# A hybrid attention block on one core: ln_g as columns, memory keys and values stored unsplit, decay sums as strips

## The chip, the cores and the metric

The kernel runs on one core of a Trainium2 chip. The metric is the device time of one execution in microseconds. Runs are compared as medians; the profile is of one further execution, taken by the hardware profiler, which has its own time. The engines are named as the profile names them: PE is TensorE (PEld its weight loads), DVE is VectorE, ACT is ScalarE, POOL is GpSimd, SP is SyncE, which only issues DMAs here.

## What is computed

One layer of a decoder over 1024 tokens of width 2048, in float32:

```
h = RMSNorm(x) * ln_g
P = h @ W_in            split into g_u g_v g_z | d_q d_k d_v d_z d_a d_b | c_q c_z
A: gMLP gating in chunks of 128;  B: gated DeltaNet, 8 heads;  C: attention into 256 memory tokens, 4 heads
m = RMSNorm(mem) * mem_norm_g;  mk, mv = split(m @ w_mem_kv)
x = x + concat(A, B, C) @ W_out;  y = RMSNorm(x) * final_g
```

Two small pieces matter here. The columns d_a and d_b of W_in are 16 in all (8 heads, two numbers for each); with them every token gets its decay and its beta: `g = -exp(a_log) * softplus(d_a + dt_bias)`, `beta = sigmoid(d_b)`. And mk, mv are made once at the start and used in the cross-attention much later, so they are stored in between.

## The kernel before

A float32 product is made of three products in the faster type fp32r: an operand is split into a high part (a cast) and a low part (the difference), and hi*hi, hi*lo and lo*hi are added in PSUM (`triple`, line 445; `split_to`, line 437, the cast on ACT and the subtraction on DVE). Transposes and a few small products use plain fp32.

The whole program is first recorded as operations (`Plan.add`, line 138) and then put in order by a planner (`Plan.issue`, line 229): each engine has a queue of what is ready, takes the lowest rank (`with rank(...)`), and prices each operation by a model (`price`, line 188). Which operation waits for which follows from the regions that they write and read (`region`, line 108); a PSUM bank counts as one region. Each engine runs its own instructions in the planned order, so all recorded lines of the trace are line 300, and groups are told apart by the names of the tiles. `together` (line 102) keeps a bundle of PE instructions in one piece. `behind(op)` makes an operation wait for another.

**Opening.** Rows of mem (256 tokens) and the first half of x (token tiles 0 to 3 of 128 tokens) are loaded with tokens in partitions, four blocks of 512 columns for a tile. `row_scale` (line 454) makes the RMS factor of each token: four squares with a running sum on ACT, 512 columns each, then DVE and POOL. `prep` (line 546) multiplies a block by that factor and by ln_g in one DVE instruction (line 551). For that ln_g lies in SBUF as four broadcasts over all partitions (`gb`, line 479, loaded at line 605 from SP's queue). PE transposes the block into a PSUM bank of the ring dn. `put0` (line 559) takes it from there: for tiles 0 and 1 ACT copies it to SBUF, it is split into `ahq`/`alq`, and the sum is written to `h0_d` in DRAM; for tiles 2 and 3 it is split straight from PSUM, and the sum is made again later from both parts and written then (`whole`, line 728, and `left_sums`, line 734).

Between these steps runs the product of the memory (lines 580 to 633): for each of 16 k, a block of w_mem_kv is loaded, scaled and split, and PE makes keys (`ka`, four banks acc0 to acc3, 256 columns each) and values (`va`, banks dn0 and dn1). At its end (lines 635 to 658) keys and values are scaled, split, and both parts stored to `kv_d` by POOL's queue.

**Tiles 4 to 7** are prepared while the first large product already runs (lines 1322 to 1333): `prep1` (line 747) leaves the transposed block unsplit in SBUF, writes part of it to `hT_d`, and `left_sums` forms sums of first and second half. Large products over 2048 columns of P follow in the rest of the program; they are made from sums of blocks, seven products for eight, in the order of `first_product` and `seven`.

**Decays.** `abw` holds the 16 columns of W_in, split into two parts of 16 columns for each k. For the second half (tiles 4 to 7) `decay_rows` (line 781) puts the 16 values of k into four strips: four fp32 matmuls with a 32-column stationary operand write to partitions 0, 32, 64 and 96 of one bank, 16 matmuls for a token tile, in one bundle. For the first half `decay_mm` (line 776) multiplies all 512 tokens with the split operands, 32 matmuls with 512 columns (lines 1326 to 1330). `decays` (line 793) transposes the result, adds the groups and makes gates and decays.

**Late.** In the cross-attention stage (lines 1733 to 1737) keys and values are read from `kv_d` in both parts, from POOL's queue, into tiles of the rings gt and inv.

Of the kernel before, what the change touches and what calls it, by code (L numbers as in the profile page):

```python
# [17 lines left out]
P = 128  # L18
D = 2048
KT = D // P  # L20
NQ = 4
# [39 lines left out]
class Plan:  # L61
# [242 lines left out]
def kernel(  # L304
# [95 lines left out]
    et = [C([P, HT], f"et{i}", F32R) for i in range(2)]  # L400
    for t in et:
        R.users[t.tensor.name] = []
    ring = {t: Slots(t, 2, [P, HT]) for t in ("kT", "qT", "vs", "kd", "ai")}
    twin = {t: C([P, 2 * HT], f"{t}w") for t in ring}
    ring |= {t: Slots(t, 2, [P, 2 * HT]) for t in ("inv", "gt")}
    ring["ut"] = Ring("ut", 2, [P, 2 * HT])
    ring["zg"] = Ring("zg", 2, [P, 2 * HT])
    zgb = ring["zg"].bufs
    ring["zg"].bufs = [b[:, i * HT : (i + 1) * HT] for b in zgb for i in range(2)]
# [4 lines left out]
    jk = C([P, HT], "jk", mybir.dt.bfloat16)  # L414
# [64 lines left out]
    gb = [ring["zg"]() for _ in range(4)]  # L479
    kvraw += [ring["ut"]() for _ in range(2)]  # L480
    mem_rows = [row_tiles("kT"), row_tiles("qT")]
    x_rows = {}

# [21 lines left out]
    with rank(2):  # L505
        load_mem(0)
        S.dma_start(mrow, mem_norm_g[0].rearrange("(c p) -> c p", p=P))
        for k in range(4):
            load_kv(k)
            if k == 1:  # L510
                load_mem(1)
# [18 lines left out]
    pt = spare()  # L530
    PE.transpose(pt[:, 0:16], mrow, ident[0:16, 0:16])
    gcol = C([P, 16], "gcol")
    with rank(1):
        V.tensor_copy(gcol, pt[:, 0:16])
# [11 lines left out]
    def prep(tt, put, bank, order=range(NQ)):  # L546
# [30 lines left out]
    kvmark = []  # L577
    mhl = [spread_mem(0)]
    warm(2)
    for k in range(KT):  # L580
# [5 lines left out]
        with rank(2):  # L586
            for sl in kv_parts(k):
# [7 lines left out]
        for h in range(NX):  # L595
            sl = slice(h * P, (h + 1) * P)
            triple(ka[h][:, :NMEM], (hi[:, sl], lo[:, sl]), (mh[:, kk], ml[:, kk]), k == 0, k == KT - 1)
        for mt in range(2):
            sl = slice(mt * P, (mt + 1) * P)
            triple(va[mt], (mh[:, kk, sl], ml[:, kk, sl]), (hi[:, XW:], lo[:, XW:]), k == 0, k == KT - 1)  # L600
        kvmark.append(R.ops[-1])
        if k == 3:
            with rank(2), behind(kvmark[-1]):
                for c in range(4):
                    Q.dma_start(gb[c], ln_g[0, c * HT : (c + 1) * HT].partition_broadcast(P))
# [29 lines left out]
    kv_d = DT([2, NX, P, 2, NMEM], "kvd")  # L635
    with rank(1):
        kfs = [t[:, i * NMEM : (i + 1) * NMEM] for t in (ring["xr"](), ring["xr"]()) for i in range(2)]
        for h in range(NX):
            V.tensor_tensor(out=kfs[h], in0=ka[h][:, :NMEM], in1=rmb, op=ALU.mult)
    for mt in range(2):  # L640
        t = [ring[("ai", "kd")[mt]](F32R) for _ in range(2)]
        with rank(1):
            S.activation(t[0], va[mt], AF.Copy, scale=rm[mt])
            V.scalar_tensor_tensor(t[1], va[mt], rm[mt], t[0], op0=ALU.mult, op1=ALU.subtract)
        for i in range(2):
            with rank(2.5):
                G.dma_start(
                    kv_d[1, :, :, i, mt * P : (mt + 1) * P].rearrange("h p e -> p h e"),
                    tok(t[i]).bitcast(F32),
                )  # L650
    with rank(2):
        prep(3, put0(3), spare, (2, 3, 0, 1))
    for h in range(NX):
        t = (ring["vs"](F32R) if h < 2 else et[h - 2]).rearrange("p (s m) -> p s m", s=2)
        with rank(2.2):
            split_to(t[:, 0], t[:, 1], kfs[h], V)
        with rank(2.5):
            G.dma_start(kv_d[0, h], t.bitcast(F32))
    et = [heir(t, f"ef{i}", f"et{i}", HT) for i, t in enumerate(et)]


    R.gate = kvmark[8]
    with rank(2.5):
# [4 lines left out]
        abf = ring["E"]()[:, 0 : KT * 16].rearrange("p (k c) -> p k c", c=16)  # L668
        G.dma_start(abf, w_in[:, C_AB : C_AB + 16].rearrange("(k p) c -> p k c", p=P))
# [7 lines left out]
    with rank(3.5):  # L677
# [9 lines left out]
        abw = C([P, KT * 32 + 96], "abw", F32R)  # L687
        R.users[abw.tensor.name] = []
        V.tensor_scalar(abw[:, KT * 32 :], ident[:, 0:96], 0.0, None, op0=ALU.mult)
        abv = abw[:, 0 : KT * 32].rearrange("p (k c) -> p k c", c=32)  # L690
        S.copy(abv[:, :, 0:16], abf)
        V.tensor_tensor(out=abv[:, :, 16:32], in0=abf, in1=abv[:, :, 0:16], op=ALU.subtract)
# [35 lines left out]
    def whole(q, tt):  # L728
        t = ring["tn"]()
        with rank(4):  # L730
            V.tensor_tensor(out=tok(t), in0=ahq[q][:, tt], in1=alq[q][:, tt], op=ALU.add)
            Q.dma_start(rows_of(h0_d, q, tt), twos_of(t))

    def left_sums(tt, q):
# [4 lines left out]
        if tt >= H0:  # L739
            Q.dma_start(rows_of(h0_d, q, tt), twos_of(a))  # L740
# [6 lines left out]
    def prep1(i):  # L747
        def put(q, tp):
            t = x_rows[NT + i][q]
            S.copy(t, tp.rearrange("p t c -> p (t c)"))  # L750
# [30 lines left out]
    def decay_rows(o, tt):  # L781

        a = work()
        with R.together():
            for q in range(NQ):
                for j in range(4):
                    k = 4 * q + j
                    PE.matmul(a[j * 32 : (j + 1) * 32, 0:P],
                              abw[:, k * 32 : (k + 1) * 32].bitcast(F32), tok(x_rows[NT + tt][q])[:, j],
                              start=q == 0, stop=q == NQ - 1)  # L790
        S.copy(o[:, tt * P : (tt + 1) * P], a[:, 0:P])

    def decays(hf, a, bank):

        NU, M = NT * NH, P if hf else 32
# [7 lines left out]
        with rank(R.cls):  # L803
            V.tensor_reduce(abt, tp[:, 0 : NT * M].rearrange("p (t g c) -> p t c g", t=NT, c=2 * NH), axis=AX.X, op=ALU.add)
# [427 lines left out]
    def right_first(m, j):  # L1232

        ts = kept1[j]
        if m == 1:
            with rank(3.3):
# [82 lines left out]
    strips, sums0 = ring["xr"].bufs[2][:, 0:HT], ring["xr"].bufs[1][0:32, 0:HT]  # L1319
    room = over([*spares.bufs, *et])  # L1320
    R.slow = 800.0
    with rank(4):
        for i in range(NT):
            prep1(i)
            decay_rows(strips, i)
            if i == 1:
                a = work()
                for k in range(KT):
                    decay_mm(a, k)
                S.copy(sums0, a[0:32])  # L1330
# [3 lines left out]
    for q in range(NQ // 2, NQ):  # L1334
        for tt in range(H0, NT):
            whole(q, tt)
# [29 lines left out]
    zh, zl = (heir(b, n, tag, 2 * HT, F32R) for b, n, tag in zip(zgb, ("zh", "zl"), ("zg0", "zg1")))  # L1366
# [4 lines left out]
    el = over([heir(abw, "el0", "abw", KT * 32 + 96)[:, 0:HT], ring["tn"].bufs.pop()])  # L1371
# [444 lines left out]
    def square(half_, t, c):  # L1816
        S.activation(jk, ys[half_][t][c], AF.Square, accum_out=ssy[half_][t][:, c : c + 1])
# [108 lines left out]
```

## Time and profile before

| | |
|---|---|
| median of 3 runs | 1592.1 us (1588.9 to 1592.44) |
| the profiled execution | 1596.31 us, its span 1594.5 us |
| granted TensorE clock in it | 0.998 |
| busy: PE, DVE, ACT, POOL | 1576.7, 1291.9, 1017.2, 311.8 us |
| moved by DMA | 428.88 MB, mean 269 GB/s |

A row of instructions gives its start, its busy time, engine, line, operation, the tiles written and read, shape and count; in brackets how long the engine stood idle before it and what ended that. Busy time of overlapping instructions is counted once in a group. A row of waits gives who waited for whom: total, times, longest. A row of DMA issues gives the queue, the count, the size of one and the median time from issue to landing.

### The profile page before, as it was taken

How to read it: one execution, taken by the hardware profiler on the slowest of the kernel's cores; microseconds unless marked ns; L12 is line 12 of the kernel's file. 1: busy time of each engine (PE TensorE's matmuls, PEld its weight loads, DVE VectorE, ACT ScalarE, POOL GpSimd, SP SyncE). 2: the span in 40 equal slices, each digit the busy share in tenths (PEclk: the TensorE clock that was granted, in tenths of full speed). 3: DMA queues.
4: the chain of work that ended last, by engine and by line, in shares of the span. 5: the costliest groups of instructions: out<-in, count | busy, mean ns of one | idle time of the engine just before them, and what ended most of it. 6: DMA issues, size and time to landing. Idle time of an engine off the chain costs nothing.

```text
span 1594.5 us, 25290 instructions
## 1 busy us (share of the span) xinstructions
PE 1576.7 (99%) x8538; PEld 1324.7 (83%) x8538; DVE 1291.9 (81%) x1977; ACT 1017.2 (64%) x2115; POOL 311.8 (20%) x514
## 2 busy tenths in 40 slices
PE   9999999999999999999999999999999999999997
PEld 8878888888888888888888888888888888888886
DVE  6978986989899998998987776767778788778776
ACT  7843675776656788866776667665646874344355
POOL 1200132332302423245232233221000000000001
PEclk9999999999999999999999999999999999999999
DMA  9988868988679868986779775799877679688646
GB/s 331 326 288 269 289 202 294 360 297 270 203 248 343 276 216 279 351 311 221 263 233 343 249 272 180 232 309 327 298 243 240 225 236 360 202 277 293 215 148 242
DMA packets 214819, 428.88 MB, mean 269 GB/s; under 512 B 23193, under 2 KB 58737, under 8 KB 214689
## 3 DMA queue, kind: packets, MB, share of 16 engines
q1 hardware_dynamic: 191184, 368.71, 68.9%
q0 software_dynamic: 22896, 57.50, 10.8%
q8 instruction: 67, 1.10, 0.3%
q10 hardware_dynamic: 608, 1.06, 0.2%
q14 instruction: 64, 0.52, 0.1%
HBM read 337.49 MB, written 89.16 MB: 268 GB/s over the span
## 4 chain that ended last, share of the span: by engine, by line
PE 90%; DMA 5%; DVE 2%; issue 1%; ACT 1%; POOL 0%; SPq 0%; POOLq 0%; DVEq 0%; ACTq 0%
PE acc L300 63%; PE dn L300 27%; DMA wraw<-in_w_in_dram 2%; DVE wlo L300 1%; DMA kT<-late 1%; DVE alo L300 0%; DMA ut<-in_w_mem_kv_dram 0%; DMA qTw<-in_x_dram 0%; DMA qTw<-sa 0%; DMA vsw<-sa 0%; DMA kTw<-in_w_in_dram 0%; SPq L300 0%; DMA wraw<-in_w_mem_kv_dram 0%; ACT whi L300 0%; DMA y<-in_w_in_dram 0%
## 5 line engine op out<-in xcount | busy, mean ns | idle before, releaser
L300 PE MATMUL acc<-ahi,whi 128*128 128x512 f32 (+1 forms) x1328 | 458.5, 393 | 0.3 <-ACT whi L300 0.3
L300 PE MATMUL acc<-ahi,wlo 128*128 128x512 f32 (+1 forms) x904 | 354.2, 392 | 0.7 <-DVE wlo L300 0.7
L300 PEld LDWEIGHTS acc<-ahi,whi 128*128 128x128 f32 x1328 | 248.3, 188 | 48.0 <-ACT whi L300 0.5
L300 ACT CAST ahi<-raws 128x1024 fp32r<-128x1024 f32 x141 | 147.8, 1048 | 82.5 <-PE dn L300 35.9
L300 PEld LDWEIGHTS acc<-ahi,wlo 128*128 128x128 f32 x904 | 170.1, 188 | 33.6 <-DVE wlo L300 1.4
L300 PE MATMUL acc<-alo,whi 128*128 128x512 f32 (+1 forms) x480 | 187.4, 390 | 0.0
L300 PE MATMUL acc<-ahi,zh 128*128 128x512 f32 x424 | 167.1, 394 | 0.0
L300 PE MATMUL acc<-ahi,zl 128*128 128x512 f32 x424 | 166.9, 394 | 0.0
L300 PE MATMUL acc<-alo,zh 128*128 128x512 f32 x424 | 166.7, 393 | 0.0
L300 ACT CAST whi<-wraw 128x1024 fp32r<-128x1024 f32 (+1 forms) x78 | 80.6, 1034 | 68.8 <-PE acc L300 37.2
L300 POOL TENSOR_TENSOR small<-small,mhalf 128x1 f32<-128x1 f32 x26 | 16.9, 658 | 507.2 <-DVE small L300 507.1
L300 DVE TENSOR_TENSOR wlo<-wraw,whi 128x1024 fp32r<-128x1024 f32 (+1 forms) x78 | 93.9, 1204 | 25.1 <-ACT whi L300 19.4
L300 DVE TENSOR_TENSOR alo<-raws,ahi 128x1024 fp32r<-128x1024 f32 x71 | 86.6, 1219 | 22.6 <-ACT ahi L300 22.4
L300 PEld LDWEIGHTS acc<-alo,whi 128*128 128x128 f32 x480 | 90.3, 188 | 16.8
L300 DVE TENSOR_TENSOR ahi<-raws,ahi 128x1024 fp32r<-128x1024 f32 x70 | 85.4, 1219 | 20.9 <-ACT ahi L300 19.4
L300 ACT CAST ahi<-y 128x1024 fp32r<-128x1024 f32 x65 | 68.2, 1049 | 42.2 <-PE dn L300 17.8
L300 DVE TENSOR_TENSOR alo<-y,ahi 128x1024 fp32r<-128x1024 f32 x65 | 79.7, 1225 | 16.6 <-ACT ahi L300 16.5
L300 PEld LDWEIGHTS acc<-ahi,zl 128*128 128x128 f32 x424 | 79.7, 188 | 15.8
L300 PEld LDWEIGHTS acc<-ahi,zh 128*128 128x128 f32 x424 | 79.9, 188 | 15.4
L300 PEld LDWEIGHTS acc<-alo,zh 128*128 128x128 f32 x424 | 79.7, 188 | 15.3
L300 PE MATMUL dn<-whi,ahi 128*128 128x512 f32 x232 | 77.6, 389 | 0.0
L300 PE MATMUL acc<-whi,ahi 128*128 128x512 f32 x216 | 73.7, 392 | 0.0
(587 smaller groups left out, 3765.7 us busy)
## 6 DMA issues: line engine op xcount, KB each, us to landing
wraw<-in_w_in_dram SPq DMA_DIRECT2D x80, 512.0 KB, 5.4
raws<-sa SPq DMA_DIRECT2D x61, 512.0 KB, 5.2
y<-in_w_in_dram SPq DMA_DIRECT2D x40, 512.0 KB, 5.6
wraw<-in_w_out_dram SPq DMA_DIRECT2D x32, 512.0 KB, 5.2
raws<-h0d SPq DMA_DIRECT2D x29, 512.0 KB, 5.5
y<-sa SPq DMA_DIRECT2D x27, 512.0 KB, 5.0
raws<-sd SPq DMA_DIRECT2D x42, 256.0 KB, 3.0
raws<-hTd SPq DMA_DIRECT2D x16, 512.0 KB, 4.7
```

The source lines that it names most:

```text
L300: o.fn(*o.args, **o.kw)
```

## The change

- **ln_g as columns.** The four broadcasts and their tiles (`zg`) go. ln_g is loaded as 16 rows beside mem_norm_g, transposed with it, and kept as 16 columns in `gcol`. `prep` multiplies a block by the token's factor alone, on DVE for tiles 2 and 3 and on ACT for the others; the transposed block is multiplied by ln_g where it leaves PSUM (`times_g`, on DVE). Tiles 2 and 3 now take the way of tiles 0 and 1, so `h0_d` is written in `put0` for all four, and `whole` and the store in `left_sums` go.
- **Decays of the first half in strips.** `abw` is plain fp32, 16 columns for each k, loaded at the start of the key and value loop. Tiles 0 and 1: strips of four matmuls for each block, from `put0`, into columns 256 to 383 of the banks acc0 and acc1, beside the keys. Tiles 2 and 3: `decay_split`, 32 fp32 matmuls over 256 columns, from both split parts. Tiles 4 to 7: the strips of each block are a bundle of their own. PSUM banks named acc are tracked by columns.
- **Keys and values unsplit in DRAM.** `kv_d` has half its size; the split is made after the late fetch.
- **Squares 1024 wide** where two blocks of a tile are neighbours in SBUF.
- Smaller: half of the first weight block is issued from ACT; the halves of that block come in the other order, and values are multiplied before keys; the first fetches for product 1 wait for the twelfth step of the memory product; `zh`, `zl` and `et` are tiles of their own.

```diff
-        if ap.space == PSUM:
+        if ap.space == PSUM and name[:3] != "acc":
             return name, 0, P, 1
...
+    def joined(ts):
+        out, i = [], 0
+        while i < len(ts):
+            w = whole_of.get(ts[i].tensor.name)
+            out.append(ts[i] if w is None else w)
+            i += 1 if w is None else 2
+        return out
+
     def row_scale(xq):
         s = small()
-        for c in range(4):
-            S.activation(jk, xq[c], AF.Square, accum_out=s[:, c : c + 1])
-        V.tensor_reduce(s[:, 4:5], s[:, 0:4], axis=AX.X, op=ALU.add)
+        parts = joined(xq)
+        for c, t in enumerate(parts):
+            S.activation(jk[:, 0 : t.shape[1]], t, AF.Square, accum_out=s[:, c : c + 1])
+        V.tensor_reduce(s[:, 4:5], s[:, 0 : len(parts)], axis=AX.X, op=ALU.add)
...
-        for sl in kv_parts(k):
-            Q.dma_start(kvraw[k % 4][:, sl], w_mem_kv[k * P : (k + 1) * P, sl])
+        for i, sl in enumerate(kv_parts(k)[::-1]):
+            (S if (k, i) == (0, 0) else Q).dma_start(kvraw[k % 4][:, sl], w_mem_kv[k * P : (k + 1) * P, sl])
...
+    def times_g(o, tp, q):
+        V.tensor_tensor(out=o, in0=tp, in1=bc(gcol[:, 16 + 4 * q : 20 + 4 * q], P), op=ALU.mult)
...
-            V.scalar_tensor_tensor(xq[q], xq[q], r, gb[q], op0=ALU.mult, op1=ALU.mult)
+            if H0 <= tt < NT:
+                V.tensor_scalar(xq[q], xq[q], r, None, op0=ALU.mult)
+            else:
+                S.activation(xq[q], xq[q], AF.Copy, scale=r)
...
+    def first_ab(tt):
+        return ka[tt][:, NMEM : NMEM + P]
+
+    def decay_rows(a, q, t, start):
+        with R.together():
+            for j in range(4):
+                k = 4 * q + j
+                PE.matmul(a[j * 32 : (j + 1) * 32], abw[:, k * 16 : k * 16 + 32], t[:, j],
+                          start=start, stop=q == NQ - 1, skip_group_check=True)
+
     def put0(tt):
         def put(q, tp):
-            if tt >= H0:
-                with rank(1):
-                    split_to(ahq[q][:, tt], alq[q][:, tt], tp, V)
-                return
             t = tok(ring["tn"]())
             with rank(1):
-                S.copy(t, tp)
+                times_g(t, tp, q)
             with rank(2):
                 split_to(ahq[q][:, tt], alq[q][:, tt], t, V)
+            if tt < H0:
+                decay_rows(first_ab(tt), q, t, False)
...
-    kv_d = DT([2, NX, P, 2, NMEM], "kvd")
+    kv_d = DT([2, NX, P, NMEM], "kvd")
...
-    def decay_mm(a, k):
-        wk = abw[:, k * 32 : k * 32 + P]
-        mm(a, wk, ahi[k], k == 0, False)
-        mm(a, wk, alo[k], False, k == KT - 1)
...
+    def decay_split():
+        a = work()[:, 0 : H0 * P]
+        with R.together():
+            for i, part in enumerate((ahi, alo)):
+                for q in range(NQ):
+                    for j in range(4):
+                        k = 4 * q + j
+                        PE.matmul(a[j * 32 : (j + 1) * 32], abw[:, k * 16 : k * 16 + 32],
+                                  part[k][:, H0:].bitcast(F32), start=i == q == 0, stop=i == 1 and q == NQ - 1)
+        S.copy(sums0[:, H0 * P :], a)
...
             prep1(i)
-            decay_rows(strips, i)
+            a = work()[:, 0:P]
+            for q in range(NQ):
+                decay_rows(a, q, tok(x_rows[NT + i][q]), q == 0)
+            S.copy(strips[:, i * P : (i + 1) * P], a)
             if i == 1:
-                a = work()
-                for k in range(KT):
-                    decay_mm(a, k)
-                S.copy(sums0, a[0:32])
+                decay_split()
...
-            G.dma_start(t, kv_d[n, 2 * i : 2 * i + 2].rearrange("h p s m -> p h s m"))
+            G.dma_start(t[:, :, 1].bitcast(F32), kv_d[n, 2 * i : 2 * i + 2].rearrange("h p m -> p h m"))
+            with rank(1.5):
+                split_to(t[:, :, 0], t[:, :, 1], t[:, :, 1].bitcast(F32), V)
```

More of the change, by code (lines that the diff above doesn't have):

```diff
@@ L399 @@
     kvhi, kvlo = [*whi.bufs], [*wlo.bufs]
-    et = [C([P, HT], f"et{i}", F32R) for i in range(2)]
-    for t in et:
-        R.users[t.tensor.name] = []
+    et = [C([P, HT], f"et{i}") for i in range(2)]
     ring = {t: Slots(t, 2, [P, HT]) for t in ("kT", "qT", "vs", "kd", "ai")}
     twin = {t: C([P, 2 * HT], f"{t}w") for t in ring}
+    whole_of = {t.tensor.name: t for t in twin.values()}
     ring |= {t: Slots(t, 2, [P, 2 * HT]) for t in ("inv", "gt")}
     ring["ut"] = Ring("ut", 2, [P, 2 * HT])
-    ring["zg"] = Ring("zg", 2, [P, 2 * HT])
-    zgb = ring["zg"].bufs
-    ring["zg"].bufs = [b[:, i * HT : (i + 1) * HT] for b in zgb for i in range(2)]
     ring["E"] = Ring("E", 2, [P, HT])
@@ L478 @@
     R.late = R.LATE
-    gb = [ring["zg"]() for _ in range(4)]
     kvraw += [ring["ut"]() for _ in range(2)]
@@ L482 @@
     x_rows = {}
+    whole_of.update((t.tensor.name, t) for t in ring["ut"].bufs)
     def load_mem(q):
@@ L507 @@
         S.dma_start(mrow, mem_norm_g[0].rearrange("(c p) -> c p", p=P))
+        S.dma_start(rows[16:32], ln_g[0].rearrange("(c p) -> c p", p=P))
         for k in range(4):
@@ L529 @@
     warm(7)
-    pt = spare()
-    PE.transpose(pt[:, 0:16], mrow, ident[0:16, 0:16])
-    gcol = C([P, 16], "gcol")
+    pt = acc[3]
+    PE.transpose(pt[:, 0:32], rows[0:32], ident[0:32, 0:32])
+    gcol = C([P, 32], "gcol")
     with rank(1):
-        V.tensor_copy(gcol, pt[:, 0:16])
+        V.tensor_copy(gcol, pt[:, 0:32])
+    def times_g(o, tp, q):
+        V.tensor_tensor(out=o, in0=tp, in1=bc(gcol[:, 16 + 4 * q : 20 + 4 * q], P), op=ALU.mult)
     def spread_mem(q):
@@ L577 @@
     kvmark = []
+    abw = C([P, HT], "abw")
+    G.memset(abw[:, KT * 16 : KT * 16 + 16], 0.0)
     mhl = [spread_mem(0)]
@@ L586 @@
         with rank(2):
-            for sl in kv_parts(k):
+            for sl in kv_parts(k)[::-1]:
                 raw = kvraw[k % 4][:, sl]
@@ L600 @@
             triple(va[mt], (mh[:, kk, sl], ml[:, kk, sl]), (hi[:, XW:], lo[:, XW:]), k == 0, k == KT - 1)
+        for h in range(NX):
+            sl = slice(h * P, (h + 1) * P)
+            triple(ka[h][:, :NMEM], (hi[:, sl], lo[:, sl]), (mh[:, kk], ml[:, kk]), k == 0, False)
         kvmark.append(R.ops[-1])
[L602 to L605, printed above, removed]
+        if k == 0:
+            with behind(kvmark[-1]), rank(2):
+                G.dma_start(abw[:, 0 : KT * 16].rearrange("p (k c) -> p k c", c=16),
+                            w_in[:, C_AB : C_AB + 16].rearrange("(k p) c -> p k c", p=P))
         if k in (1, 4, 8):
@@ L633 @@
                 prep(2, put0(2), spare, (2, 3, 0, 1))
-    kv_d = DT([2, NX, P, 2, NMEM], "kvd")
+    kv_d = DT([2, NX, P, NMEM], "kvd")
     with rank(1):
-        kfs = [t[:, i * NMEM : (i + 1) * NMEM] for t in (ring["xr"](), ring["xr"]()) for i in range(2)]
+        kfs = [t[:, i * NMEM : (i + 1) * NMEM] for t in et for i in range(2)]
         for h in range(NX):
             V.tensor_tensor(out=kfs[h], in0=ka[h][:, :NMEM], in1=rmb, op=ALU.mult)
+    for h in range(NX):
+        with rank(2.5):
+            G.dma_start(kv_d[0, h], kfs[h])
     for mt in range(2):
-        t = [ring[("ai", "kd")[mt]](F32R) for _ in range(2)]
+        t = ring[("ai", "kd")[mt]]()
         with rank(1):
[L643 to L650, printed above, removed]
+            S.activation(t, va[mt], AF.Copy, scale=rm[mt])
+        with rank(2.5):
+            G.dma_start(kv_d[1, :, :, mt * P : (mt + 1) * P].rearrange("h p e -> p h e"), tok(t))
     with rank(2):
         prep(3, put0(3), spare, (2, 3, 0, 1))
[L653 to L659, printed above, removed]
+    sums0 = ring["xr"].bufs[1][:, 0:HT]
+    with rank(2):
+        for tt in range(H0):
+            S.copy(sums0[:, tt * P : (tt + 1) * P], first_ab(tt))
     R.gate = kvmark[8]
@@ L686 @@
             V.tensor_copy(col2, pt[:, 96:105])
[L687 to L692, printed above, removed]
     states = C([P, NH * P], "states")
@@ L726, in blk @@
         return w[k * P : (k + 2) * P, c0 : c0 + HT].rearrange("(u p) c -> p u c", u=2)
[L728 to L732, printed above, removed]
     def left_sums(tt, q):
@@ L749, in put @@
             t = x_rows[NT + i][q]
-            S.copy(t, tp.rearrange("p t c -> p (t c)"))
+            times_g(tok(t), tp, q)
             if q >= NQ // 2:
@@ L774 @@
     scan_banks, work = dnr.bufs[0:2], over(dnr.bufs[2:4])
-    def decay_mm(a, k):
-        wk = abw[:, k * 32 : k * 32 + P]
-        mm(a, wk, ahi[k], k == 0, False)
-        mm(a, wk, alo[k], False, k == KT - 1)
-    def decay_rows(o, tt):
-        a = work()
-        with R.together():
[L785 to L791, printed above, removed]
+    def decay_split():
+        a = work()[:, 0 : H0 * P]
+        with R.together():
+            for i, part in enumerate((ahi, alo)):
[5 more added lines that the diff above has]
+        S.copy(sums0[:, H0 * P :], a)
     def decays(hf, a, bank):
-        NU, M = NT * NH, P if hf else 32
+        NU, M = NT * NH, P
         ab = a
@@ L1235, in right_first @@
         if m == 1:
-            with rank(3.3):
+            with rank(3.3), behind(kvmark[11]):
                 fetch(ts, first_block(0, 0, j))
@@ L1318 @@
                     Q.dma_start(tiles[i][c], x[(NT + i) * P : (NT + i + 1) * P, c * HT : (c + 1) * HT])
-    strips, sums0 = ring["xr"].bufs[2][:, 0:HT], ring["xr"].bufs[1][0:32, 0:HT]
+    strips = ring["xr"].bufs[2][:, 0:HT]
     room = over([*spares.bufs, *et])
@@ L1365 @@
     wraw2 = over([*kvraw[:2], more[1]])
[L1366 removed]
+    zh, zl = (C([P, 2 * HT], n, F32R) for n in ("zh", "zl"))
     whi3, wlo3 = over([*kvhi, zh]), over([*kvlo, zl])
@@ L1370 @@
     cross = over([heir(b, f"utc{i}", f"ut{i}", 2 * HT, F32R) for i, b in enumerate(ring["ut"].bufs)])
-    el = over([heir(abw, "el0", "abw", KT * 32 + 96)[:, 0:HT], ring["tn"].bufs.pop()])
+    el = over([abw, ring["tn"].bufs.pop()])
     wide = acc
```

17 lines of the change are left out of this document (3 added, 14 removed).

## Prediction

> **What bounds the kernel now.** I read the page first, then the waits of TensorE, then the opening by windows, because every edit but one acts there.
>
> ```profile
> span 1594.5 us, 25290 instructions
> PE 1576.7 (99%) x8538; PEld 1324.7 (83%) x8538; DVE 1291.9 (81%) x1977; ACT 1017.2 (64%) x2115; POOL 311.8 (20%) x514
> ```
> ```profile
> PE dn L300 <- ACT vs L300: 1.7, 1, 1.7
> PE dn L300 <- DVE whi L300: 1.4, 1, 1.4
> ```
> ```profile
> PE dn L300 <- ACT jk L300: 1.3, 1, 1.3
> PE dn L300 <- ACT tn L300: 0.9, 1, 0.9
> PE acc L300 <- ACT ahi L300: 0.8, 1, 0.8
> PE acc L300 <- DVE wlo L300: 0.4, 1, 0.4
> PE acc L300 <- ACT whi L300: 0.3, 1, 0.3
> ```
> ```profile
> 0.00:45.00 45.00, 42.10 (x267) 37.94 (x268) 29.50 (x48) 34.31 (x67) 7.63 (x19) 0.96 0.96 328
> 45.00:90.00 45.00, 41.35 (x292) 37.07 (x294) 38.51 (x70) 36.36 (x83) 8.22 (x14) 1.00 0.95 322
> 90.00:135.00 45.00, 45.00 (x332) 36.21 (x333) 33.18 (x58) 17.32 (x33) 2.51 (x4) 1.00 0.87 278
> ```
> TensorE is the bound almost everywhere: 17.8 us of 1594.5 are idle (1594.5 - 1576.7). The first wait list is of the whole span, the second of 40 to 90 us; in the windows the columns are PE, PEld, DVE, ACT, POOL busy, the clock, the DMA share and GB/s. Two things can therefore move the end: TensorE work added or removed (it is full from 90 us on, so a microsecond counts as one), and the five named waits of 40 to 90 us, together 1.3 + 0.9 + 0.8 + 0.4 + 0.3 = 3.7 us. In that window DVE (38.5 of 45), ACT (36.4 of 45) and the DMA engines (0.95) are all close to full, so the waits come from there.
>
> **TensorE work, part by part.** The decays of the first four token tiles were 32 matmuls over 512 columns, in one stretch, with two groups of transposes among them:
>
> ```profile
> 99.61 0.50 PE L300 MATMUL dn<-ahi,abw 128*128 128x512 f32 x1
> ...
> 101.54 0.60 PE L300 MATMUL dn<-ident,gt 128*128 128x128 f32 x4
> 101.90 0.48 PE L300 MATMUL dn<-ahi,abw 128*128 128x512 f32 x1
> 102.21 0.39 PE L300 MATMUL dn<-alo,abw 128*128 128x512 f32 x1
> ...
> 108.00 0.40 PE L300 MATMUL acc<-ahi,wlo 128*128 128x512 f32 x1
> ```
> From 99.61 to 108.00 are 8.39 us. A transpose group takes 101.54 to 101.90, 0.36 us, and the matmul behind it starts its successor 0.31 instead of 0.23 us later, so 0.44 for each of two: **-7.5 us** for what goes. What comes instead has the form of the strips that tiles 4 to 7 already use, four 32-column strips of the array side by side:
>
> ```profile
> 89.59 0.39 PE L300 MATMUL acc<-ahi,whi 128*128 128x512 f32 x1
> 89.91 0.64 PE L300 MATMUL dn<-kdw,abw 128*32 128x128 f32 x16
> 90.37 0.62 PE L300 MATMUL dn<-vsw,abw 128*32 128x128 f32 x16
> 90.92 0.66 PE L300 MATMUL dn<-ident,ut 128*128 128x128 f32 x4
> ...
> 92.81 0.60 PE L300 MATMUL dn<-ident,ut 128*128 128x128 f32 x4
> ```
> The profile counts an fp32 matmul as two instructions: 16 matmuls of one tile are the x16 and the x16. Half a tile takes 90.37 - 89.91 = 0.46 us, a tile 0.92. The matmul before it started at 89.59 and would have had a successor at 89.82 by the pitch of 0.23 above; the strips start 0.09 later, and leaving costs 0.09 again (90.92 - 90.37 - 0.46). So a **visit** to this form costs 0.18 us beside its matmuls.
> - decay_split, tiles 2 and 3: 32 strip matmuls over 256 columns, so twice the count and twice the length of a tile's 0.92, 3.7, and one visit: **+3.9**.
> - Tiles 0 and 1, now strips inside the key and value loop: 2 x 0.92, and a visit for each of their 8 blocks, since each block's bundle is its own: 8 x 0.18. **+3.3**. They could be nearly free if they fell into waits, but the waits there are too short and few (one of 0.9) to count on that.
> - Tiles 4 to 7: the 16 matmuls of a tile, one bundle before, become four bundles that are ready one after the other. Bounds: 0 if they still go out together, 12 more visits, 2.2, if not. Blocks of a tile come to TensorE apart (the transposes of 90.92 and 92.81 above, with other products between), and the bundles' rank sends them out when ready: **+2.2**.
> - The transposes of the first half's sums have 128 rows instead of 32: between 0 and one transpose group, 0.44; I take **+0.2**.
>
> Sum on TensorE: -7.5 + 3.9 + 3.3 + 2.2 + 0.2 = **+2.1 us**. What the 32 long matmuls give up, the visits of the short strips take back.
>
> The page "TensorEngine Tiling (Array Packing)" of the Trainium skill, section Key Properties, says that changing the tiling mode drains TensorE. The 0.18 us of a visit agrees with a drain in kind but is short; what a full one would make of the sum is the fourth rival.
>
> **Waits of the opening.** What held ACT ahead of three of the five waits were transfers that landed late:
>
> ```profile
> 46.97 0.63 ACT L300 ACTIVATE jk<-kTw 128x512 bf16<-128x512 f32 x1 [1.79 <-DMA kTw<-in_x_dram]
> ...
> 64.08 0.63 ACT L300 ACTIVATE jk<-qTw 128x512 bf16<-128x512 f32 x1 [2.38 <-DMA qTw<-in_x_dram]
> ...
> 83.02 0.83 ACT L300 CAST whi<-wraw 128x768 fp32r<-128x768 f32 x1 [2.80 <-DMA wraw<-in_w_in_dram]
> ```
> ```profile
> h0d<-tn SPq DMA_DIRECT2D x12, 256.0 KB, 5.0
> zg<-in_ln_g_dram SPq DMA_DIRECT2D x4, 256.0 KB, 7.4
> kvd<-ai POOLq DMA_DIRECT2D x2, 256.0 KB, 7.2
> ```
> ```profile
> 18.39 3.84 SPq L300 DMA_DIRECT2D zg<-in_ln_g_dram  x4
> ```
> The list of issues covers 0 to 100 us; kvd has three more rows like the one shown (from kd, vs, et), 8 stores in all. The four broadcasts of ln_g go: 4 x 256 KB are 1.05 MB, 3.3 us at the 322 GB/s of the window, and 3.84 us of SP's own time, behind which the next weight block and the x rows of tile 1 stood. The stores of keys and values halve: another 1.05 MB, 3.3 us, ahead of the block that landed at 83. Against that, all 16 h0 stores are now issued from the preparation of tiles 0 to 3 instead of 12 within 100 us, so up to 4 x 256 KB, 3.3 us, come forward. Net: 3.3 us less queue, more than any one of the three landings was late (1.79, 2.38, 2.80). The abw fetch moves ahead of these, from the POOL queue as before, 128 KB, and is needed only at tile 0's first strip.
>
> On DVE, whose ring of work decides the other two:
>
> ```profile
> 6.28 0.49 DVE L300 TENSOR_SCALAR whi<-wraw,gcol 128x512 fp32r<-128x512 f32 x1 [1.56 <-DMA wraw<-in_w_mem_kv_dram]
> ...
> 60.31 0.68 DVE L300 TENSOR_TENSOR tn<-ahi,alo 128x512 f32<-128x512 f32 x1
> ...
> 63.57 1.41 DVE L300 TENSOR_TENSOR xr<-acc,E 128x256 f32<-128x256 f32 x4
> ...
> 70.38 1.41 DVE L300 SCALAR_TENSOR_TENSOR qTw<-qTw,small,zg 128x512 f32<-128x512 f32 x2 [0.50 <-POOL small L300]
> ```
> Tiles 2 and 3, eight blocks: a scaling of 0.49 and a times_g priced as the 0.68 of a 512-wide tensor_tensor replace 0.71 (half of 1.41): 8 x 0.46 = +3.7. Gone are four sums in whole (4 x 0.68), the two halves of the values' split (2 x 0.71) and four 256-wide subtractions for the keys (four such took 1.41): -5.5. Net -1.8 us; tiles 0, 1 and 4 to 7 swap one operation for one. ACT takes over the scalings of six tiles but gives up the copies out of PSUM and two of the squares' fixed parts; I count it as even. So I take the five waits as gone: **-3.7 us**, with 0 as the other bound.
>
> **What is hidden.** At the start, half of key block 0 is issued from ACT; the wait of 1.4 <- DVE whi also has DVE's own work in it, so 0 to -1.4, I take 0. The values go first in each block; only which half of the last block is late changes. The late split of keys and values (four 512-wide pairs on ACT and DVE, not two stores' worth of loads) lies under slack:
>
> ```profile
> 880.00:900.00 20.00, 18.31 (x85) 14.76 (x84) 11.77 (x16) 11.07 (x19) 7.75 (x11) 1.00 1.00 327
> ```
> DVE and ACT have 8 of 20 us free where the values are fetched; without that cover each pair would cost its 0.68 and a like time on ACT, 2.7 to 5 us for four. The gate on the fetch of m = 1 holds back 128 KB early, a gain in the queue. The order of everything later is made anew from changed costs and buffers; I count it as 0, and give it 2 us to either side, about the size of the largest single wait (1.7).
>
> **Sum.** +2.1 - 3.7 = **-1.6 us**. The profiled execution took 1596.3, so 1594.7 for one like it; the median of the runs shown is 1592.1, so **1590.5**.
>
> **Rivals.**
> 1. Visits cost nothing and the start gains: strips go out together or in waits, -7.5 + 3.7 + 1.8 + 0.2 = -1.8, all five waits gone, -3.7, and the 1.4 at the start too: -6.9, **1585.2**. For it: adjoining half tiles follow one another without a gap (89.91, 90.37). Against: blocks come apart.
> 2. The transfers are hidden anyway: SP mostly waits for buffers, not bandwidth, then no wait goes and TensorE's +2.1 stands: **1594.2**.
>
> ```profile
> SPq L300 <- DVE wlo L300: 14.6, 9, 3.8
> ```
> In 0 to 110 us that is SP's longest wait. Against: the broadcasts alone are 3.84 us of SP.
>
> 3. Slower: the hand-over to the first product. Keys now end last in each block, so the four scalings out of PSUM (1.41 in all) no longer lie under the value products, and the strips of tiles 0 and 1 share banks 0 and 1 with the keys; and tile 3 gets a further DVE step for each of four blocks (4 x 0.68 = 2.7) before the second half of the first product can begin, where TensorE already waits 0.8 for ahi. With +2.1 and no wait gone: 2.1 + 1.4 + 2.7 = +6.2, **1598.3**. It decides if DVE stays as full between 60 and 75 us as now. The page "PSUM — Partial Sum Buffer" of the Trainium skill, section Terms, says that two engines must not touch one bank and quadrant at once, which would turn sharing of banks into waiting; no run here shows it yet.
> 4. Each visit costs a full drain: a matmul's own 0.39 against the pitch of 0.23 is 0.16, going in and coming out 0.32 instead of 0.18; for 21 more visits (8, 12 and 1) +2.9: -1.6 + 2.9 = +1.3, **1593.4**. Against it stand the measured gaps. The page on tiling named above would give this one.
>
> **How the numbers follow.** 0.3% is 4.8 us, about what a measurement of this kernel can tell from no change. Forecast 0.42, rival 1 0.25, rival 2 0.12, rival 3 0.16, rival 4 0.05. Only rival 1 is faster by more than 4.8, and a little of the forecast's spread: 0.28. Slower: rival 3 and a little of the spread: 0.18. Same: 0.54. The range goes from rival 1 less 2 us of reordering, 1583, to rival 3, 1598. The forecast's own range is 1587 to 1594.
>
> **What would show it.** TensorE: abw groups over 512 columns gone, a group of 128*32 over 256 columns of some 3.7 us, bundles of 8 instructions with 0.1 to 0.2 us around each. Waits of 40 to 90 us: jk, tn, ahi, whi and wlo gone or under 0.3 each. The second tile's landing wait on ACT (1.79) gone. The forecast is wrong if the five waits stay, if a wait on xr or et keys appears at the first product, or if visits cost under 0.05 or over 0.3 us.

## The result, and the profile after

The changed kernel took **1602.1 us** (median of 6 runs, 1601.2 to 1606.7) beside 1591.4 us for the kernel before on the same chip: ratio **1.0069, interval 1.0057 to 1.0080**. It is slower by some 11 us; the prediction said 1590.5 and a range up to 1598.

The page of the changed kernel, its span and busy times:

```profile
span 1600.4 us, 25403 instructions
...
PE 1586.8 (99%) x8634; PEld 1323.6 (83%) x8634; DVE 1294.0 (81%) x1977; ACT 1017.6 (64%) x2088; POOL 309.8 (19%) x513
```

TensorE's idle time fell from 17.8 to 13.6 us (1600.4 - 1586.8), but its busy time grew by 10.1 us (1586.8 - 1576.7). So no new wait is to blame: instructions take longer, or there are more of them. The waits of TensorE in the whole span (who waited for whom: total, times, longest), the whole list:

```profile
PE dn L300 <- DMA abw<-vd: 1.3, 2, 1.1
PE dn L300 <- POOL ones L300: 1.1, 1, 1.1
PE dn L300 <- DMA kT<-in_mem_dram: 0.6, 1, 0.6
PE dn L300 <- DVE whi L300: 0.4, 1, 0.4
PE dn L300 <- DVE tn L300: 0.3, 1, 0.3
```

Of the five waits that were to go (jk, tn, ahi, wlo, whi in 40 to 90 us) none is left but 0.3 us on tn. The opening by windows (PE, PEld, DVE, ACT, POOL busy, clock, DMA share, GB/s):

```profile
0.00:45.00 45.00, 42.88 (x276) 37.38 (x277) 26.98 (x44) 32.64 (x57) 7.85 (x21) 1.00 0.89 290
45.00:90.00 45.00, 44.65 (x340) 39.97 (x340) 37.91 (x68) 36.24 (x64) 7.56 (x11) 1.00 1.00 348
90.00:135.00 45.00, 45.00 (x377) 34.20 (x376) 34.87 (x65) 18.83 (x35) 1.30 (x4) 1.00 0.77 250
```

Where the opening ends, at 217 us, TensorE is 2.4 us **ahead** of the profile of before (the 900th of the matmuls over 256 or 512 columns that both kernels have starts at 217.4, before at 219.8; about half of that is the clock of the first 20 us, below). From there on the lead melts evenly: 0.9 us ahead at 355, 0.3 behind at 492, 1.5 behind at 780, 4.1 behind at 1569. The second profile of the kernel before, shown below, starts this matmul at 217.3, so the lead is no more than two profiles of one kernel differ; against it the changed kernel is 0.1 us behind at 217, 1.5 at 355, 2.8 at 492, 3.8 at 780 and 8.8 at 1569. A loss spread over the whole span is no single event; it points to a price on each of many instructions. The groups by line and shape (busy, mean ns of one, idle before) show which. Before:

```profile
L300 PE MATMUL acc<-ahi,whi 128*128 128x512 f32 x1312 | 454.0, 395 | 0.0
L300 PE MATMUL acc<-ahi,zh 128*128 128x512 f32 x424 | 167.1, 394 | 0.0
L300 PE MATMUL acc<-ahi,zl 128*128 128x512 f32 x424 | 166.9, 394 | 0.0
```

And after:

```profile
L300 PE MATMUL acc<-ahi,whi 128*128 128x512 f32 x1312 | 454.4, 395 | 0.0
...
L300 PE MATMUL acc<-ahi,zh 128*128 128x512 f32 x424 | 169.3, 399 | 0.0
L300 PE MATMUL acc<-ahi,zl 128*128 128x512 f32 x424 | 169.0, 399 | 0.0
L300 PE MATMUL acc<-alo,zh 128*128 128x512 f32 x424 | 168.9, 398 | 0.0
```

(A name "acc<-ahi,zh" is: result, streamed operand, weights.) The same 424 instructions with the same operands take 5 ns more if zh or zl is an operand, and nothing more if whi is. In the timeline the pitch, start to start, shows it better than the mean of one. Fourteen products in a row with zh and zl, first and last; before:

```profile
302.07 0.39 PE L300 MATMUL acc<-ahi,zh 128*128 128x512 f32 x1
...
305.02 0.39 PE L300 MATMUL dn<-alo,zh 128*128 128x512 f32 x1
```

after:

```profile
300.57 0.40 PE L300 MATMUL acc<-ahi,zh 128*128 128x512 f32 x1
...
303.61 0.39 PE L300 MATMUL dn<-alo,zh 128*128 128x512 f32 x1
```

Thirteen steps take 2.95 us before and 3.04 after: 227 and 234 ns. What the change did to zh and zl is small: before, they were heirs of the ln_g tiles zg0 and zg1; as these are gone, they became tiles of their own and got another place in SBUF.

### The profile page after: what moved, and what is told of

Its sections match the earlier page's. It is cut to its first block, busy times and chain, and to the rows that moved or that the text cites. A ratio compares the mean times of both kernels' runs of the same rounds, so it can differ in the third digit from the quotient of the medians.

```text
span 1600.4 us, 25403 instructions
## 1 busy us (share of the span) xinstructions
PE 1586.8 (99%) x8634; PEld 1323.6 (83%) x8634; DVE 1294.0 (81%) x1977; ACT 1017.6 (64%) x2088; POOL 309.8 (19%) x513
## 4 chain that ended last, share of the span: by engine, by line
PE 96%; DMA 1%; DVE 1%; ACT 1%; issue 1%; ACTq 0%; POOLq 0%; POOL 0%; DVEq 0%; SPq 0%
PE acc L300 68%; PE dn L300 28%; DMA y<-in_w_in_dram 1%; DMA abw<-vd 0%; DMA wraw<-in_w_mem_kv_dram 0%; DMA y<-h0d 0%; DVE wlo L300 0%; DVE y2w L300 0%; ACT ahi L300 0%; DVE alo L300 0%; ACT y2w L300 0%; DVE vs L300 0%; ACT zh L300 0%; ACT utl L300 0%; ACT whi L300 0%
```

## Experiments

The kernels in the table issue the same instructions in the same order on every engine as the changed kernel (or, where said, as the kernel before); only byte addresses differ. The addresses, from the built programs (one partition's bytes; ahi, alo, whi, wlo lie at 128 modulo 256, except where said):

```
                      zh at byte   mod 256   off the other split operands, mod 256
before                 139,392      128         0
after                  219,072      192        64
e1_zh_low              139,392      128         0
e5_zh_256              139,648      128         0
e6_zh_512              139,904      128         0
e2_zh_low_phase        140,288        0       128
e3_zh_mid              173,824        0       128
e8_before_zg_phase     140,288        0       128   (kernel before)
e4_shift_all           139,520        0         0   (kernel before, all tiles 128 up)
```

**The kernel before once more**, unchanged, as the measure for the traces of that chip.

> The kernel before, unchanged, for a profile on the same chip: pitch of matmuls with zh or zl 227-228 ns, with gt and inv as weights 233; the span some us under the 1594.5 of the profile shown, as its median is.

It took 1591.5 us, span 1589.7, pitch of the zh products 227.8 ns. Its span is 4.8 us shorter than that of the first profile of the same kernel. Some 1.2 us of it lie in the first 20 us, whose windows (the clock is the third number from the end) read so in the first profile and in this one:

```profile
0.00:20.00 20.00, 17.10 (x98) 15.46 (x99) 8.85 (x14) 11.15 (x21) 1.28 (x9) 0.91 0.88 307
```
```profile
0.00:20.00 20.00, 17.29 (x105) 15.41 (x106) 9.14 (x16) 11.67 (x21) 1.43 (x9) 1.00 0.88 312
```

So differences of a few us between two single traces are no evidence, and the verdicts below go by medians and by pitches.

**zh and zl back at their old place**, all else as changed:

```diff
     ring["ut"] = Ring("ut", 2, [P, 2 * HT])
+    zhl = [C([P, 2 * HT], n, F32R) for n in ("zh", "zl")]
...
-    zh, zl = (C([P, 2 * HT], n, F32R) for n in ("zh", "zl"))
+    zh, zl = zhl
```

> The changed kernel, whose instructions are the same in kind and order on every engine; only the place of zh and zl in SBUF differs: they lie where the ln_g broadcasts lay (byte 139,392 of a partition), not behind everything else (219,072). Theory P (place): the start-to-start time of 512-column matmuls that use zh or zl as weights falls from 233 to 227-228 ns, about 1250 matmuls by 5.6 ns, 7 us: 1595, ratio to before 1.002 to 1.004. Rival W (work): the changed order and the strips cost the 11 us, the place nothing: 1602, ratio 1.007.

1592.1 us against 1593.5 for the kernel before: ratio **0.9994, 0.9985 to 1.0003**. The whole loss is gone. Its page and the group of zh:

```profile
span 1591.7 us, 25403 instructions
...
PE 1576.2 (99%) x8634; PEld 1322.1 (83%) x8634; DVE 1292.2 (81%) x1977; ACT 1015.8 (64%) x2088; POOL 307.9 (19%) x513
```
```profile
L300 PE MATMUL acc<-ahi,zh 128*128 128x512 f32 x424 | 167.1, 394 | 0.0
```

The median is 10.1 us under the changed kernel's (1602.1 - 1592.1, on two chips). The span is 8.7 us shorter (1600.4 - 1591.7), with the same instructions, and 8.6 of that come after 217 us.

**Is it the neighbourhood or the offset?** Two kernels put zh and zl close to the old place, 896 bytes higher, and in the middle of SBUF, both 128 bytes off the others modulo 256. The edit is the one above, with one difference each: in the first kernel the small rings hs and small now come ahead of zh and zl, in the second the line that makes zh and zl stands behind many other tiles.

> As the run before, but the two small rings hs and small lie in front, so that zh starts at 140,288: still in the low part, but at another offset within 2048 bytes (1024 instead of 128, which whi, wlo, ahi and alo have). Theory P1 (height in the partition decides): 227-228 ns as in the run before, about 1595. Theory P2 (offset against the other operand decides): 233 ns, about 1602.

> zh and zl at 173,824 and 177,920, next to the rings gt and inv, which in the kernel before were slow weights too (233 ns). P1: slow, 232-233 ns and about 1602, if the boundary lies below; P2: the offset within 2048 bytes is 1792, so slow as well. If it is fast, the boundary lies between 177,920 and 219,072 and gt and inv are slow for another reason.

1600.7 us, ratio 1.0043 (1.0029 to 1.0058), and 1603.1 us, ratio 1.0059 (1.0042 to 1.0075). The groups of zh in the first and in the second:

```profile
L300 PE MATMUL acc<-ahi,zh 128*128 128x512 f32 x424 | 169.3, 399 | 0.0
```
```profile
L300 PE MATMUL acc<-ahi,zh 128*128 128x512 f32 x424 | 169.3, 399 | 0.0
```

Between 896 bytes and 80 KB (the changed kernel) from the good place the group's mean is the same, 399 ns. So it is the offset, not the neighbourhood. The ratios, 1.0043 to 1.0069, spread more than that; their intervals overlap or just touch.

**Of what period, and against what?** One execution each, read by the pitch: zh 256 and 512 bytes above the old place, and the kernel before with 128 unused bytes ahead of all its tiles.

> The changed kernel with zh and zl low, but 256 bytes further than in the good place (139,648). If the period is 256 or less: 227-228 ns. If it is 512 or more (the bytes of one row of 128 columns of weights): 232-233 ns.

> The same, 512 bytes further than the good place (139,904). If the period is 512 or less: 227-228 ns, 1593; if it is 1024 or more: 232-233 ns, about 1600.

> The kernel before, with the same instructions in the same order, and 128 unused bytes ahead of all its tiles: every offset moves by 128, so weights and streamed operands keep their distance from each other. If only the distance between the two operands counts (theory R, relative), all pitches stay: 227-228 ns for whi and zh, 233 for gt and inv; 1592. If the offset itself counts (theory A, absolute: 128 within some power of two is the good one), all large matmuls go to 232-233 ns: some 6000 by 5.5 ns, 33 us slower, 1625.

1593.6, 1591.6 and 1590.6 us; pitch of the zh products 227.7, 227.8 and 227.9 ns. So 256 bytes are a whole period, and an offset that all operands have costs nothing: what counts is a difference between weights and streamed operand. Mean start-to-start times in ns, worked out from the traces (two neighbouring matmuls over 512 columns without a wait between them, 170 to 1600 us; streamed operand, weights):

```
                        before  e1     e2     e3     e8     after
ahi,zh then alo,zh      227.8   227.8  233.2  233.2  233.2  233.3
ahi,wlo then ahi,whi    227.7   227.8  227.9  227.8  227.9  228.1
zh,ahi then zl,ahi      227.1   227.2  232.8  232.8  232.8  232.2
zl,ahi then zh,alo      226.7   226.6  232.5  232.5  232.5  227.4
```

Whether it must be the two operands of one and the same matmul the runs do not settle. Where the weights change, in e8, "ahi,zl then ahi,whi" takes 233.3 ns, but "ahi,wlo then ahi,zh" takes 232.7 too (76 times; 227.9 in the kernel before), although ahi and wlo lie alike. With 64 bytes, in the changed kernel, the latter takes 227.7.

**The place alone, without any of the change.** The kernel before, its tiles zg0 and zg1 made 896 bytes higher:

```diff
     ring["ut"] = Ring("ut", 2, [P, 2 * HT])
+    ring["hs"] = Ring("hs", 4, [P, 10, NT])
+    small = Ring("small", 8, [P, 8])
     ring["zg"] = Ring("zg", 2, [P, 2 * HT])
...
-    ring["hs"] = Ring("hs", 4, [P, 10, NT])
...
-    small = Ring("small", 8, [P, 8])
```

> The kernel before, with nothing of the change in it; only the tiles zg0 and zg1 (and so zh and zl, their heirs) lie 896 bytes higher, 128 bytes off the other split operands modulo 256. Theory (the places of the operands alone cost the time): the products with zh or zl go from a pitch of 228 to 233 ns, about 1800 of them, +5.5 ns each, so +9 to +10 us, ratio 1.005 to 1.007. Rival (the place costs only together with the changed order of the new kernel): ratio 1.000, pitch 228.

1602.6 us against 1592.5: ratio **1.0063, 1.0042 to 1.0083**. Nothing but the place of zg0 and zg1 (with zh and zl) and of the small tiles around them makes the kernel before as slow as the changed one. Its page and group:

```profile
span 1600.2 us, 25290 instructions
...
PE 1585.1 (99%) x8538; PEld 1325.9 (83%) x8538; DVE 1294.6 (81%) x1977; ACT 1019.1 (64%) x2115; POOL 317.5 (20%) x514
```
```profile
L300 PE MATMUL acc<-ahi,zh 128*128 128x512 f32 x424 | 169.2, 399 | 0.0
```

The count agrees too. zh or zl are the weights of 1356 matmuls over 512 columns and the streamed operand of 456. In this run the mean pitch of the first is 232.7 instead of 227.7 ns, of the second 232.8 instead of 227.0: 1356 x 5.0 ns and 456 x 5.8 ns are 6.8 + 2.6 = 9.4 us. The medians differ by 10.1; the span is 10.5 us over that of the second profile of the kernel before, 9.1 of it after 217 us (in the first 20 us this execution had a granted clock of 0.91, that one 1.00). In the changed kernel the weights lose 5.6 ns (233.3), the streamed ones only 2.8 (229.7), so 7.6 + 1.3 = 8.9, against 8.7 between its span and that of the version with zh at the old place.

**Is there more of this to gain?** In the kernel before gt and inv, too, lay 64 bytes off, and as weights under ahi and alo ran at 234.5 and 233.4 ns from 83 to 165 us beside 228.5 and 228.8 for whi and wlo; with zh low they lie 128 off, at 231.9 and 232.7. This kernel is the changed one with zh, zl, gt, inv and the small fp32 operands all at 128 modulo 512. The order in which tiles are made does most of it; gcol and rm also become columns of abw, and six of TensorE's instructions come out in another order.

> The changed kernel with zh and zl low, and with the other tiles that TensorE reads (ident, ones, gt, inv, kT, qT, states, steps, wsbt) at 128 within 512 bytes too: gcol and rm inside abw, xr behind ident, wsbt and abt moved; the order of the instructions stays. Theory: gt and inv as weights fall from 232-233 to 227-228 ns for 512 columns, about 190 matmuls, 1 us, and their 256-column matmuls of the memory product (some 770) by up to 3 ns, 2 us: 1588 to 1591, ratio 0.997 to 0.999. Rival: their slowness has another cause; then as with zh and zl low alone, 0.9994.

1592.1 us against 1593.3: ratio 0.9996, 0.9985 to 1.0007. gt and inv as weights fell to 229.1 and 229.0 ns there. Over the whole span 234 matmuls have them as weights, and their mean goes from 232.3 with zh low to 230.4: half a microsecond, too little to be seen in the time. The 256-column products of the memory stayed at 117 to 120 ns, whether gt and inv lay 64, 128 or 0 bytes off.

**What ln_g as columns does**, with zh at its old place: ln_g again as four broadcasts, multiplied in by DVE, ACT copying out of PSUM.

```diff
+    ring["zg"] = Ring("zg", 2, [P, 2 * HT])
...
-            if H0 <= tt < NT:
-                V.tensor_scalar(xq[q], xq[q], r, None, op0=ALU.mult)
-            else:
-                S.activation(xq[q], xq[q], AF.Copy, scale=r)
+            V.scalar_tensor_tensor(xq[q], xq[q], r, gb[q], op0=ALU.mult, op1=ALU.mult)
...
-        V.tensor_tensor(out=o, in0=tp, in1=bc(gcol[:, 16 + 4 * q : 20 + 4 * q], P), op=ALU.mult)
+        S.copy(o, tp)
```

> The changed kernel with zh and zl at their old place and ln_g again as four broadcasts, multiplied in by DVE with the token's factor; the copy out of PSUM is ACT's again. Theory that the broadcasts made the opening's waits: in 40 to 90 us TensorE's waits go from 0.9 back to 2 us or more, and the landing wait on ACT ahead of the second tile comes back; time 1 to 2.5 us above the aligned version. Rival (the halved stores of keys and values made the gain): waits stay near 0.9 and the time does not move. Second rival (ln_g as columns costs DVE more than it gives): waits under 0.9, time lower by 1 us or more.

1594.6 us, ratio 1.0017 (1.0002 to 1.0032); the version with zh at its old place alone, which the expectations of this and the next kernel call the aligned one, had 0.9994. The intervals just touch. TensorE's waits of 40 to 90 us:

```profile
PE dn L300 <- ACT tn L300: 1.7, 1, 1.7
PE dn L300 <- ACT kdw L300: 1.0, 1, 1.0
PE acc L300 <- DVE et L300: 0.2, 1, 0.2
```

They were 0.9 in the version with zh low (ahi 0.6, tn 0.3) and are 2.9 here. But the landing wait on ACT ahead of the second tile (its squares over kTw) did not come back. What TensorE waits for here are ACT's copies out of PSUM (tn, kdw). That the broadcasts' transfers had made the waits is not borne out. This kernel brings back the broadcasts and the old split of the work between ACT and DVE together, so what each of them does it cannot say.

**One bundle for each of tiles 4 to 7**, zh at its old place: the four bundles of a tile written as one, as before.

```diff
-            for q in range(NQ):
-                decay_rows(a, q, tok(x_rows[NT + i][q]), q == 0)
+            with R.together():
+                for q in range(NQ):
+                    for j in range(4):
+                        k = 4 * q + j
+                        PE.matmul(a[j * 32 : (j + 1) * 32], abw[:, k * 16 : k * 16 + 32], tok(x_rows[NT + i][q])[:, j],
+                                  start=q == 0, stop=q == NQ - 1, skip_group_check=True)
```

> The changed kernel with zh and zl at their old place, and the strips of each of the tiles 4 to 7 in one bundle again, not four. By the visits' measured price (0.22 us, some 4 to 5 visits fewer): TensorE work -1 us, time -1 us against the aligned version if nothing waits for the last block instead; 0 if the later bundle holds back what follows. By the prediction's count of 12 visits: -2.2 us.

1596.4 us, ratio **1.0026** (1.0016 to 1.0036): slower, where 1 us less was expected. The strips did get cheaper: all of them together take 11.7 us of TensorE's time beyond their neighbours' pitch, 12.7 with four bundles. At 149 us TensorE was 2.6 us ahead of the version with four bundles. Then it waited; the timeline of PE around the wait, and the window:

```profile
162.43 0.47 PE L300 MATMUL dn<-ahi,wlo 128*128 128x512 f32 x1
166.66 0.79 PE L300 MATMUL acc<-ahi,whi 128*128 128x512 f32 x1 [3.75 <-ACT whi L300]
167.25 0.63 PE L300 MATMUL acc<-alo,whi 128*128 128x512 f32 x1
167.68 0.63 PE L300 MATMUL acc<-ahi,whi 128*128 128x512 f32 x1
168.10 0.63 PE L300 MATMUL acc<-alo,whi 128*128 128x512 f32 x1
...
171.51 0.59 PE L300 MATMUL acc<-ahi,wlo 128*128 128x512 f32 x1
171.94 0.39 PE L300 MATMUL dn<-ahi,whi 128*128 128x512 f32 x1
```
```profile
165.00:175.00 10.00, 8.34 (x26) 6.64 (x27) 8.28 (x15) 4.06 (x7) 0.00 (x0) 0.66 0.99 355
```

The split weights come late. The cast that TensorE waits for, in ACT's timeline:

```profile
165.77 0.83 ACT L300 CAST whi<-wraw 128x768 fp32r<-128x768 f32 x1 [1.15 <-DVE wraw L300]
```

ACT itself stood idle 1.15 us for a sum that DVE had still to make, and DVE, busy 9.8 of the 10 us from 145 and 8.8 of those from 155, was at the sums and the decays. In the version with four bundles ACT makes this cast at 162.35; here casts of zh, of the other whi and two of ahi (160.96 to 163.48) go ahead of it. After a gap of 3.75 us the granted clock is halved for 5 us: a pitch of 0.43 instead of 0.23 us. The page "TensorE: Matmul & The Clock Gate" of the Trainium skill, section 'Part 1: The HAM clock gate (the "warmup" mystery)', says that an idle window of about 3.4 us takes the clock to half; the trace agrees, here after 3.75 us. The twelve matmuls that start from 166.66 on, up to 171.94, take 5.28 us where twelve steps of 0.23 would have taken 2.8. So the wait and its after-effect, 3.75 + 2.5, are 6.3 us, more than the lead. The edit changed the planner's order of everything that follows, so this run is no clean price of a visit: TensorE was 2.1 us ahead just before the wait and the weights came later than in the version with four bundles, so only a part of the wait is the lead.

## Why the prediction was wrong

**The step that failed** is the one on what is hidden: "The order of everything later is made anew from changed costs and buffers; I count it as 0, and give it 2 us to either side". What failed in it is the buffers' part: of zh and zl becoming tiles of their own nothing was costed, and no rival had it. It measured **+8.7 us** between the spans of two kernels with the same instructions in the same order, and 10.1 us between medians, both in the changed kernel and in the kernel before. The new order, with zh and zl at the old place, shows no loss (0.9994). The prediction took one pitch of 0.23 us for every matmul over 512 columns; before's own trace had two, 228 to 229 ns for whi and wlo and 232 to 235 for gt, inv and abw as weights, and to ask why was the way to this result.

The rest of the prediction was about the kernel with zh at its old place, and against that it can be held. Its sum was -1.6 us; measured are -0.06% (-0.15% to +0.03%), that is -1.0 us of 1593.5, and 1.4 us between the medians. The interval holds zero, and that the size fits is partly luck: by the steps below TensorE's work was forecast some 1.2 us too high and the gain from the waits 1.2 us too high, and the two cancel. By its steps, from the traces of the changed kernel:

- **The long matmuls, -7.5**: gone. **The strips of tiles 0 and 1 and decay_split** came as described:

```profile
34.05 0.40 PE L300 MATMUL dn<-whi,inv 128*128 128x512 f32 x1
34.37 0.43 PE L300 MATMUL acc<-tn,abw 128*32 128x128 f32 x8
34.73 0.55 PE L300 MATMUL dn<-ident,vsw 128*128 128x128 f32 x3
...
104.22 0.42 PE L300 MATMUL dn<-ut,abw 128*32 128x128 f32 x8
104.46 1.91 PE L300 MATMUL dn<-ahi,abw 128*32 128x256 f32 x32
106.19 1.91 PE L300 MATMUL dn<-alo,abw 128*32 128x256 f32 x32
108.03 0.66 PE L300 MATMUL dn<-ident,gt 128*128 128x128 f32 x4
```

  A bundle of 8: 34.73 - 34.37 = 0.36, of which a quarter of 0.92 is work, so 0.13 at one end; at the other 34.37 - 34.05 less a pitch of 0.23, 0.09. A visit of so short a bundle is **0.22**, not 0.18. decay_split took 108.03 - 104.46 = 3.57, and had no visit of its own, since it went out with a bundle of tile 5: 3.6, not 3.9.
- **Tiles 4 to 7, +2.2**: taken at the upper bound, and wrong there. Tile 4 went out as 32 instructions at once, tile 5 as 8, 16 and 8 (the last with decay_split), tiles 6 and 7 as 24 and 8: four more visits, not twelve, about 0.9. All strips together cost 8.2 us more than before's four (12.7 and 4.5 beyond the neighbours' pitch), where the steps made 9.4. So TensorE's work came out at about +0.7 to +1, not +2.1.
- **The waits, -3.7**: right in size in the changed kernel (0.3 us left); in the version with zh low 0.9 are left, beside 3.4 in the kernel before on that chip, -2.5. The reason given was only partly right. The issues of 0 to 100 us show the stores as described:

```profile
h0d<-tn SPq DMA_DIRECT2D x16, 256.0 KB, 5.5
kvd<-et POOLq DMA_DIRECT2D x4, 128.0 KB, 6.4
kvd<-ai POOLq DMA_DIRECT2D x1, 256.0 KB, 6.0
```

  and the landing wait of the second tile's squares is gone. But another landing wait is there on ACT between 40 and 90 us, `jk <- ut`, of 1.6 us, and TensorE waits for nothing behind it; and with the broadcasts back, TensorE's waits came from ACT's copies.
- **The late split, 0**: no wait on the keys and values shows in TensorE's list above. The start and the transposes of 128 rows are below what two single traces can tell.
- **Rivals.** The second (no wait goes) and the third (a wait at the first product, on xr or et) are out: those waits are not there. The time of the first (1585.2) was not reached by any version. The fourth, a full drain for each visit, gave 0.32; measured 0.22. The page "TensorEngine Tiling (Array Packing)" of the Trainium skill, Key Properties, says that a change of tiling mode drains TensorE; the trace agrees that the change costs something, 0.22 us there and back.

No version here beats the kernel before by more than its interval. The change without the misplaced tiles is neutral within 0.15%: what the opening gains is at most a microsecond or two.

## What to carry to other kernels

Moving a buffer is an edit with a price: before calling a change of allocation free, write down the byte offset, modulo 256, of both SBUF operands of the matmuls that run most often, and keep them equal (shown here for fp32r over 512 columns). A loss that grows evenly over the whole span points to a price on each instruction: compare the mean and the start-to-start time of the same group before and after, ahead of any search for waits. And a lead won in one stage is only kept if the next stage's operands come in time; here 2.6 us won early ended in a wait of 3.75 us and a halved clock, because the planner's new order also brought the next weights later.

## What the runs showed of the hardware

- **Operands at different offsets.** Matmuls over 512 columns (fp32r) with weights and streamed operand at the same offset modulo 256 bytes follow one another every 227 to 228 ns; 64 or 128 bytes off it is 232 to 234 ns. Moving both by 128 bytes, or one by 256 or 512, changes nothing. Other differences than 0, 64 and 128 were not tried, and why it is so no run shows: the rows give the price, not the mechanism. In the changed kernel, with 64 bytes, part of the matmuls with zh or zl streamed ran at 227.4; with 128 bytes these ran at 232.5. The products over 256 columns of the memory showed no such price (117 to 120 ns).
- The page "TensorE: Matmul & The Clock Gate" of the Trainium skill, section "Wait — 56ns, not 53.3ns?", has a start-to-start of N / 2.4 GHz + 2.5 ns, which for 512 columns is 215.7 ns. The rows here stand at 227 and 233 at a granted clock of 1.00. The measurement decides.
- A gap of 3.75 us ahead of TensorE was followed by 5.3 us at half clock, so it cost 3.75 + 2.5 = 6.3 us.
